# Memory keys and values of the second layer as one pair, with two seven-product places

## The chip, the cores and the metric

The kernel runs on one core of a Trainium2 chip. Its metric is the device time of one execution in microseconds, smaller is better, given as the median of several runs. The engines of the core are TensorE (PE: matmuls, and PEld: loads of the stationary operand), VectorE (DVE), ScalarE (ACT), GpSimd (POOL) and SyncE (SP, which here only issues DMAs). Matmuls write into PSUM, eight banks of 128 partitions by 512 fp32; everything else lies in SBUF or in the chip's memory.

## What is computed

The kernel is a decoder trunk of two layers for 256 tokens of width 2048. Both layers attend, besides their own mixer, to 256 memory tokens. The part that matters here is the projection of the normalized memory into keys and values, once for each layer:

```python
mem_n = rmsnorm(mem, norm_mem)
for i in range(DEPTH):                       # DEPTH = 2
    mk, mv = split_cols(mem_n @ mem_w_kv[i], [512, 512])   # mem_n 256x2048, each half 2048x512
    h = rmsnorm(x, norm_mix[i])
    x = x + mixer_i(h, mk, mv, ...)          # gated linear attention, then forgetting attention
    x = x + conv_ffn(rmsnorm(x, norm_ffn[i]), ...)
```

All of it is in fp32. TensorE gets each fp32 factor as a high and a low half, and a product is three matmuls: high by high, low by high, high by low.

## The kernel before

**Panels and units.** Every projection is cut into panels of at most 512 output columns. A panel has 16 blocks of 128 input features, loaded two at a time: a unit is 128 partitions by 2 x 512 weights (512 KB). For one unit TensorE runs 12 matmuls: two token halves, two feature blocks, three each. `proj_tm` (L235) runs one panel: `split_unit` (L211) loads a unit into `raw` (four buffers), ACT copies it to the high half `whi` (L208), DVE subtracts to get the low half `wlo` (L217; three buffers of each half), and `products` (L221) writes the matmuls of L229, L230 and L233. They collect in two `acc` banks out of a pool of four (L148), one for each token half, and after the last unit a panel's `evac` reads the banks.

**Pairs and seven-product places.** `proj_seven` (L270) runs two panels over the same input together, on all four banks, unit by unit in turn. At the units named in `forms` it takes the two units of the two panels as a 2 x 2 block problem (two token halves and two feature blocks, two panels) and uses seven products where eight would stand. It needs sums and differences of the weights (`t13` and `t24`, four DVE instructions, L338 to L341), their high and low halves (L312, L313), and sums of the tokens, made ahead (`summed`, L1022 to L1031). Three of the seven products go straight into `acc` banks, four into the work banks `m1`, `m5`, `m6`, `m7`, which are the kernel's `t`, `s` (two) and `o` banks, and `more` adds these up. All matmuls of a pair are written by `emit` (L286, the matmul is L291). Before the change only the down projections of the feed-forward do so, eight pairs with 20 places in all (`SEVEN`, L40).

**The memory stage.** L644 to L671 run four panels one after another on the memory tokens (`bufA`): keys and values of the first layer, then keys and values of the second, each by `proj_tm`. `keys` (L631) sends a panel through `to_features` (L420: scaled copy by ACT, transpose by DVE at L394, and two trips through memory); `mv_out` (L641) sends one through `to_values` (L442, the scaled copy is L449). The scales come from the memory norm: its squares are summed on tiles `x[0]` and `x[1]` (L646 to L654), a small matmul (L511) and a chain of short DVE instructions (L513 to L531, Newton steps at L519 to L522) follow when the norm is first asked for, at the evacuation of the first layer's values. Between the panels stand the 16 token splits for the next stage (L663, `split` at L468: an ACT copy with a gain, L478, and a DVE subtract, L479, from `xf` into `bufB`), the loads of the residual stream (`xtok` into `x`, L667, four of 512 KB) and its squares on ACT (`nx.add`, L559). After the stage the first panel of the gated linear attention (`gv`, 400 columns) reads `bufB` in order, two blocks a unit.

**What sets the order.** Each engine runs a fixed list. A planner writes the lists: it simulates the kernel and gives each engine at each moment the ready instruction of highest priority, which is that of the source, except that weight loads, casts and subtracts stand 300 places ahead (`AHEAD`, L39). `later` and `passed` (L178, L183) hang small steps on the count of units that have gone by, and `issue_after` holds a block behind a given instruction of the same engine (L665: behind the last weight load so far).

Of the kernel before, what the change touches and what calls it, by code (L numbers as in the profile page):

```python
# [19 lines left out]
P = 128  # L20
# [20 lines left out]
LAST = ()  # L41

# [95 lines left out]
def _trunk(ctx: ExitStack, tc: tile.TileContext, xt, xtok, memt, wp, wgu, gns, gfin, cnv, par, msk, out):  # L138
# [131 lines left out]
    def proj_seven(keys, src, forms, evacs, pool, more, early=False):  # L270

        units = [where[k] for k in keys]
        count = len(units[0])
        base = min(min(u[1]) for u in units[0])
        acc = [[pacc.tile([P, 512], F32, name="acc", tag="acc") for _ in range(2)] for _ in keys]
        m1, m5, m6, m7 = (work(t, n) for t, n in (("t", 1), ("s", 2), ("o", 1), ("s", 2)))
        begun, calls = set(), {}

        def form(a, x, hi, lo, c):
            s = slice(c * 512, (c + 1) * 512)  # L280
            out = []
            for xs, w in ((x[0], hi), (x[1], hi), (x[0], lo)):
                out.append((a, xs, w[:, s]))
            return out

        def emit(groups):  # L286
            todo = [g[n] for n in range(2) for g in groups] + [g[2] for g in groups]
            for a, x, w in todo:
                k = id(a)
                calls[k] -= 1  # L290
                TE.matmul(a, x, w, start=k not in begun, stop=calls[k] == 0)  # L291
                begun.add(k)
# [8 lines left out]
        for a in (m1, m5, m6, m7, acc[0][0], acc[1][0], acc[0][1]):  # L301
            count_calls(a, 3 * len(forms))
# [4 lines left out]
        def halves(raw, w):  # L307
            if w == NUNIT:
                hi, lo = (wpool.tile([P, w], F32R, name=n, tag=n, bufs=3) for n in ("whi", "wlo"))
            else:  # L310
                hi, lo = (pool.tile([P, w], F32R, name=n, tag=n) for n in ("vhi", "vlo"))
            casts.append(S.activation(hi, raw, AF.Copy))  # L312
            V.tensor_tensor(lo, raw, hi.bitcast(F32), ALU.subtract)  # L313
            return hi, lo

        def load(unit):
            off, kcs, n = unit
            raw = wpool.tile([P, NUNIT], F32, name="raw", tag="raw", bufs=4)
            loads.append(nc.sync.dma_start(raw, wp[off : off + P * NUNIT].rearrange("(p n) -> p n", p=P)))
            return raw  # L320

        for u in range(count):
            k0, k1 = units[0][u][1]
            if u not in forms:
                for i in range(2):
                    hi, lo = split_unit(units[i][u])
                    emit([form(acc[i][b], token(kc, b), hi, lo, c) for b in range(2) for c, kc in enumerate((k0, k1))])
                    if u == count - 1:
                        for b in range(2):
                            evacs[i](b, acc[i][b])  # L330
                if u == count - 2 and count - 1 in forms:
                    evacs[1](1, acc[1][1])
                continue
            s = forms[u]
            with tc.high_priority(offset=AHEAD + 40):
                r0, r1 = (load(units[i][u]) for i in range(2))
                t13, t24 = (pool.tile([P, 2, 512], F32, name=n, tag=n) for n in ("t13", "t24"))
                V.tensor_tensor(t13[:, 0, :], r1[:, :512], r0[:, :512], ALU.subtract)  # L338
                V.tensor_tensor(t13[:, 1, :], r1[:, 512:], r1[:, :512], ALU.subtract)
                V.tensor_tensor(t24[:, 0, :], r1[:, 512:], t13[:, 0, :], ALU.subtract)  # L340
                V.tensor_tensor(t24[:, 1, :], r0[:, 512:], t24[:, 0, :], ALU.subtract)  # L341
            with tc.high_priority(offset=AHEAD):
                v0 = halves(r0, NUNIT)
                v1 = halves(r1[:, 512:], 512)
            passed()
            emit([form(m1, token(k0, 0), *v0, 0), form(acc[0][0], token(k1, 0), *v0, 1)])
            emit([form(acc[1][0], s(3), *v1, 0)])
            with tc.high_priority(offset=AHEAD):
                v2 = halves(t13.rearrange("p c n -> p (c n)"), NUNIT)
            emit([form(m5, s(0), *v2, 0), form(m7, s(2), *v2, 1)])  # L350
            with tc.high_priority(offset=AHEAD):
                v3 = halves(t24.rearrange("p c n -> p (c n)"), NUNIT)
            passed()
            emit([form(m6, s(1), *v3, 0), form(acc[0][1], token(k1, 1), *v3, 1)])
            if u == count - 1:
                for i, b in ((0, 0), (1, 0), (0, 1)):
                    evacs[i](b, acc[i][b])
            if early and u == max(forms):
                more(m1, m5, m6, m7)

        if not early:
            more(m1, m5, m6, m7)

# [56 lines left out]
    def to_features(scales, dst, *steps):  # L420
# [3 lines left out]
        def evac(b, a):  # L424
# [3 lines left out]
            for k0, k1, s in scales:  # L428
# [3 lines left out]
                if s is None:  # L432
                    S.activation(o, i, AF.Copy)
                else:
                    S.activation(o, i, AF.Copy, scale=s()[:, b : b + 1])
            held[0].put(b, e)
# [5 lines left out]
    def to_values(norm, width, dst, more=None):  # L442
# [4 lines left out]
        def evac(b, a):  # L447
            e = tp.tile([P, 512], F32, name="scaled", tag="scaled", bufs=2)
            S.activation(e[:, :width], a[:, :width], AF.Copy, scale=norm.col()[:, b : b + 1])  # L449
            held.append(e)  # L450
# [158 lines left out]
    with tc.tile_pool(name="load", bufs=1) as lp:  # L609
# [46 lines left out]
        with tc.issue_after(loads[-1].ins):  # L656
            for i in range(KC):
                nc.sync.dma_start(xf[i], xt[i])
            nc.sync.dma_start(part, par)
            nc.sync.dma_start(mask[:, M_SCAN:], msk[:, M_SCAN:M_FOX])  # L660
        proj_tm(("mv", 0), bufA, mv_out(0))
        for i in range(KC):
            split(bufB, i, xf[i], gain("mix0", i), False)  # L663
        proj_tm(("mk", 1), bufA, keys(1))
# [6 lines left out]
        proj_tm(("mv", 1), bufA, mv_out(1))  # L671
# [295 lines left out]
    def add_seven(key, f, src, forms, pool, then=None):  # L967
# [13 lines left out]
        proj_seven([(*key, g) for g in (f, f + 1)], src, forms, [add_panel(g, then) for g in (f, f + 1)], pool, more,  # L981
                   then is not None)

    def ffn(l, nx, h, m, then, ending=None):
        with tc.tile_pool(name=f"ffn{l}", bufs=1) as fp, ExitStack() as ends:
# [11 lines left out]
            held = []  # L997

# [23 lines left out]
            def summed(form):  # L1022
                h0, h1 = (natural(h) for h in held)
                held.clear()
                f = sp.tile([P, 4, P], F32, name="sf", tag="sf")
                V.tensor_tensor(f[:, 0, :], h0[:, :, 1], h1[:, :, 1], ALU.add)
                V.tensor_tensor(f[:, 2, :], h0[:, :, 0], h0[:, :, 1], ALU.subtract)
                V.tensor_tensor(f[:, 1, :], f[:, 0, :], h0[:, :, 0], ALU.subtract)
                V.tensor_tensor(f[:, 3, :], h1[:, :, 0], f[:, 1, :], ALU.subtract)
                S.activation(form[:, 0, :, :], f, AF.Copy)  # L1030
                V.tensor_tensor(form[:, 1, :, :], f, form[:, 0, :, :].bitcast(F32), ALU.subtract)  # L1031
# [20 lines left out]
            for p, (lo, hi) in enumerate(PARTS):  # L1052
# [8 lines left out]
                if p < len(PARTS) - 1:  # L1061
                    for f, at in zip((0, 2), SEVEN):
                        add_seven(key, f, m, {u: form(forms[u]) for u in at}, sp)
                    continue
                if LAST:
                    add_seven(key, 0, m, {u: form(forms[u]) for u in LAST}, sp, then)
# [167 lines left out]
```

## Time and profile before

| what | value |
|---|---|
| median of 3 runs | 2243.26 us (2242.03 to 2243.55) |
| the profiled execution | 2244.32 us |
| its span, first to last instruction | 2242.5 us |
| mean granted TensorE clock | 0.999 |
| the four memory panels on TensorE | 5.37 to 95.53 us |
| of these, the second layer's keys and values | 51.43 to 95.53 us |

In the rows of the profile times are us from the start of the span unless marked ns. A row of a timeline has start, duration, engine, line, operation, output<-inputs, stationary and moving shapes, count, and in brackets the idle time before it with what ended it. A row of the groups has busy time and mean duration in ns of one instruction, and the idle time of the engine ahead of them. `wlo<-raw,whi` is a low half, `whi<-raw` a high half, `acc<-whi,A` a matmul on memory tokens, `acc<-whi,B` one on `bufB`. The duration of a matmul reaches into that of the next, so the pace is read from the starts.

### The profile page before, as it was taken

How to read it: one execution, taken by the hardware profiler on the slowest of the kernel's cores; microseconds unless marked ns; L12 is line 12 of the kernel's file. 1: busy time of each engine (PE TensorE's matmuls, PEld its weight loads, DVE VectorE, ACT ScalarE, POOL GpSimd, SP SyncE). 2: the span in 40 equal slices, each digit the busy share in tenths (PEclk: the TensorE clock that was granted, in tenths of full speed). 3: DMA queues.
4: the chain of work that ended last, by engine and by line, in shares of the span. 5: the costliest groups of instructions: out<-in, count | busy, mean ns of one | idle time of the engine just before them, and what ended most of it. 6: DMA issues, size and time to landing. Idle time of an engine off the chain costs nothing.

```text
span 2242.5 us, 29514 instructions
## 1 busy us (share of the span) xinstructions
PE 2229.0 (99%) x10276; PEld 1861.9 (83%) x10276; DVE 1631.0 (73%) x2553; ACT 1288.8 (57%) x1910; POOL 2.9 (0%) x15
## 2 busy tenths in 40 slices
PE   9999999999999999999999999999999999999998
PEld 7888888888888888888888998888888888888886
DVE  7568887667689677886776556666777967797766
ACT  7555666556565566555655555555665455654654
POOL 0000000000000000000000000000000000000000
PEclk9999999999999999999999999999999999999999
DMA  9876667677876777668787986677776678766774
GB/s 320 276 237 189 202 201 229 202 239 242 256 222 200 244 236 244 210 205 249 237 250 249 260 265 205 179 247 236 249 247 208 206 241 243 240 197 229 238 242 150
DMA packets 303773, 516.97 MB, mean 231 GB/s; under 512 B 178556, under 2 KB 187272, under 8 KB 303496
## 3 DMA queue, kind: packets, MB, share of 16 engines
q1 hardware_dynamic: 124296, 427.24, 59.1%
q10 hardware_dynamic: 179328, 87.85, 14.0%
q8 instruction: 80, 1.31, 0.3%
q14 instruction: 69, 0.57, 0.1%
HBM read 470.44 MB, written 44.58 MB: 230 GB/s over the span
## 4 chain that ended last, share of the span: by engine, by line
PE 96%; DMA 1%; DVE 1%; issue 0%; ACT 0%; SPq 0%; ACTq 0%; DVEq 0%
PE acc L229 26%; PE acc L230 26%; PE acc L233 26%; PE acc L291 12%; PE ps_s L291 1%; PE ps_o L291 1%; PE ps_t L291 1%; DMA xturned<-square 1%; PE ps_s L785 0%; DVE wlo L217 0%; PE ps_t L575 0%; PE ps_s L586 0%; PE ps_o L597 0%; DMA mt<-memt 0%; DMA raw<-wp 0%
## 5 line engine op out<-in xcount | busy, mean ns | idle before, releaser
L217 DVE TENSOR_TENSOR wlo<-raw,whi 128x1024 fp32r<-128x1024 f32 (+4 forms) x769 | 921.4, 1201 | 503.4 <-ACT whi L208 459.7
L208 ACT ACTIVATE whi<-raw 128x1024 fp32r<-128x1024 f32 (+4 forms) x769 | 799.0, 1041 | 741.1 <-PE acc L230 528.3
L229 PE MATMUL acc<-whi,B 128*128 128x512 f32 (+3 forms) x1536 | 586.2, 383 | 0.6 <-ACT whi L208 0.6
L230 PE MATMUL acc<-whi,B 128*128 128x512 f32 (+3 forms) x1536 | 584.9, 382 | 0.0
L229 PE MATMUL acc<-whi,A 128*128 128x512 f32 x1184 | 462.5, 392 | 0.9 <-ACT whi L208 0.6
L230 PE MATMUL acc<-whi,A 128*128 128x512 f32 x1184 | 461.2, 391 | 0.0
L233 PE MATMUL acc<-wlo,B 128*128 128x512 f32 (+3 forms) x1536 | 400.7, 381 | 0.0
L229 PEld LDWEIGHTS acc<-whi,B 128*128 128x128 f32 x1536 | 288.2, 188 | 51.5 <-ACT whi L208 1.1
L230 PEld LDWEIGHTS acc<-whi,B 128*128 128x128 f32 x1536 | 287.9, 188 | 49.7
L233 PEld LDWEIGHTS acc<-wlo,B 128*128 128x128 f32 x1536 | 285.6, 188 | 49.8
L233 PE MATMUL acc<-wlo,A 128*128 128x512 f32 x1184 | 318.5, 390 | 0.3 <-DVE wlo L217 0.3
L229 PEld LDWEIGHTS acc<-whi,A 128*128 128x128 f32 x1184 | 222.1, 188 | 49.2 <-ACT whi L208 2.4
L233 PEld LDWEIGHTS acc<-wlo,A 128*128 128x128 f32 x1184 | 222.1, 188 | 46.9 <-DVE wlo L217 0.7
L230 PEld LDWEIGHTS acc<-whi,A 128*128 128x128 f32 x1184 | 222.2, 188 | 46.1 <-DVE A L479 0.4
L1010 ACT ACTIVATE cv<-u,cw 128x256 f32<-128x256 f32 x176 | 96.8, 588 | 21.0 <-DMA u<-turned 21.0
L291 PE MATMUL acc<-whi,B 128*128 128x512 f32 x392 | 102.9, 390 | 0.3 <-ACT whi L208 0.3
L291 PE MATMUL acc<-whi,A 128*128 128x512 f32 x392 | 103.0, 390 | 0.0
L1011 DVE SCALAR_TENSOR_TENSOR cv<-u,cw,cv 128x256 f32<-128x256 f32 x176 | 78.4, 480 | 12.9 <-ACT cv L1010 12.9
L291 PEld LDWEIGHTS acc<-whi,B 128*128 128x128 f32 x392 | 73.5, 188 | 16.4 <-ACT whi L208 0.8
L291 PEld LDWEIGHTS acc<-whi,A 128*128 128x128 f32 x392 | 73.5, 188 | 16.1 <-ACT whi L208 0.4
L312 ACT ACTIVATE whi<-t 128x1024 fp32r<-128x1024 f32 x40 | 42.4, 1061 | 69.0 <-DVE t L341 35.3
L394 DVE STREAM_TRANSPOSE square<-scaled 128x512 f32<-128x512 f32 x122 | 79.9, 691 | 0.0
(231 smaller groups left out, 1604.0 us busy)
## 6 DMA issues: line engine op xcount, KB each, us to landing
raw<-wp SPq DMA_DIRECT2D x743, 512.0 KB, 4.3
turned<-square ACTq DMA_DIRECT2D x61, 512.0 KB, 4.3
u<-turned ACTq DMA_DIRECT2D x176, 128.0 KB, 5.1
raw<-wp SPq DMA_DIRECT2D x32, 384.0 KB, 3.5
raw<-wp SPq DMA_DIRECT2D x24, 388.0 KB, 4.6
back<-xturned ACTq DMA_DIRECT2D x64, 128.0 KB, 5.3
xturned<-square ACTq DMA_DIRECT2D x12, 512.0 KB, 4.0
back<-turned ACTq DMA_DIRECT2D x32, 128.0 KB, 4.6
```

The lines of the kernel that those rows point to most:

```text
L208: casts.append(S.activation(hi[:, s], raw[:, s], AF.Copy))
L217: V.tensor_tensor(lo[:, s], raw[:, s], hi[:, s].bitcast(F32), ALU.subtract)
L229: TE.matmul(acc[:, :n], xh, hi[:, s], start=first and j == 0, stop=False)
L230: TE.matmul(acc[:, :n], xl, hi[:, s], start=False, stop=False)
L233: TE.matmul(a, xh, ls, start=False, stop=stop)
L291: TE.matmul(a, x, w, start=k not in begun, stop=calls[k] == 0)
L312: casts.append(S.activation(hi, raw, AF.Copy))
L394: V.transpose(self.square[:, :, :, b], src.rearrange("p (c t) -> p c t", t=32))
L1010: S.activation(r, v[:, 2:], AF.Identity, bias=w[3], scale=w[2])
L1011: V.scalar_tensor_tensor(r, v[:, 1 : T + 1], w[1], r, ALU.mult, ALU.add)
```

## The change

The keys and values of the second layer no longer run as two panels but as one pair through `proj_seven`, with seven-product places at units 3 and 6 (`MEM_SEVEN`). A new `seven_evacuated` adds up the four work banks into SBUF after the last place, and the two evacuations add the sums by one DVE multiply-add for each bank, behind the scaled copy. `sums_of` makes the token sums of a place from the memory tokens, and is hung on the second and third unit of the pair. The scratch tiles are found rather than added where possible: high and low halves of the half unit in `bufB[15]` and `bufB[14]`, the two token sums in `bufB[10]` to `bufB[13]`, `t13` and `t24` in the tiles that later hold the second layer's keys and values; five tiles of 128x512 are new. Since six tiles of `bufB` are lent, the token splits 10 to 15 move behind the pair. The residual loads and their squares, which stood between the two panels, now stand ahead of the pair. `proj_seven` itself is made general (any width `n`, tiles from a callable) and takes the four work banks at the first place instead of at the start; `summed` and the new helper share `token_sums`.

```diff
+MEM_SEVEN = (3, 6)
...
-    def proj_seven(keys, src, forms, evacs, pool, more, early=False):
+    def proj_seven(keys, src, forms, evacs, tiles, more, early=False):
...
-        m1, m5, m6, m7 = (work(t, n) for t, n in (("t", 1), ("s", 2), ("o", 1), ("s", 2)))
...
+        shared = []
...
+            if not shared:
+                shared += [work(t, m) for t, m in (("t", 1), ("s", 2), ("o", 1), ("s", 2))]
+                for a in shared:
+                    count_calls(a, 3 * len(forms))
+            m1, m5, m6, m7 = shared
...
+    def seven_evacuated(keys, src, forms, evacs, tiles):
+
+        n = where[keys[0]][0][2]
+        extra = {}
+
+        def more(m1, m5, m6, m7):
+            u, v, w = (tiles(t, F32)[:, :n] for t in ("s16", "s165", "s1675"))
+            m1, m5, m6, m7 = (m[:, :n] for m in (m1, m5, m6, m7))
+            S.activation(u, m1, AF.Copy)
+            V.tensor_tensor(u, u, m6, ALU.add)
+            V.tensor_tensor(v, u, m5, ALU.add)
+            V.tensor_tensor(u, u, m7, ALU.add)
+            V.tensor_tensor(w, u, m5, ALU.add)
+            extra.update({(0, 0): m1, (1, 0): v, (0, 1): u, (1, 1): w})
+
+        def evac(i):
+            return lambda b, a: evacs[i](b, a, extra[i, b])
+
+        proj_seven(keys, src, forms, [evac(i) for i in range(2)], tiles, more, True)
+
+    def sums_of(src, chunks, f, h, form):
+
+        for c, k in enumerate(chunks):
+            V.tensor_tensor(h[:, c, :], *(src[k][:, i, :].bitcast(F32) for i in range(2)), ALU.add)
+        (a0, a1), (b0, b1) = ([h[:, c, b * P : (b + 1) * P] for b in range(2)] for c in range(2))
+        token_sums(a0, a1, b0, b1, f, form)
+
+    def token_sums(a0, a1, b0, b1, f, form):
+        V.tensor_tensor(f[:, 0, :], a1, b1, ALU.add)
+        V.tensor_tensor(f[:, 2, :], a0, a1, ALU.subtract)
+        V.tensor_tensor(f[:, 1, :], f[:, 0, :], a0, ALU.subtract)
+        V.tensor_tensor(f[:, 3, :], b0, f[:, 1, :], ALU.subtract)
+        hi, lo = form
+        S.activation(hi, f, AF.Copy)
+        V.tensor_tensor(lo, f, hi.bitcast(F32), ALU.subtract)
...
-        def evac(b, a):
+        def evac(b, a, extra=None):
...
+                    if extra is not None:
+                        V.scalar_tensor_tensor(o, extra, s()[:, b : b + 1], o, ALU.mult, ALU.add)
...
         proj_tm(("mv", 0), bufA, mv_out(0))
-        for i in range(KC):
-            split(bufB, i, xf[i], gain("mix0", i), False)
-        proj_tm(("mk", 1), bufA, keys(1))
+        for i in range(KC - taken):
+            tokens(i)
         with tc.issue_after(loads[-1].ins):
             for f in range(4):
                 nc.sync.dma_start(x[f], xtok[f])
         for f in range(4):
             for b in range(2):
                 nx.add(f, b)
-        proj_tm(("mv", 1), bufA, mv_out(1))
+        later(*[(2 + i, sums_at(u)) for i, u in enumerate(MEM_SEVEN)])
+        seven_evacuated([("mk", 1), ("mv", 1)], bufA, {u: picked(forms[u]) for u in MEM_SEVEN},
+                        [keys(1), mv_out(1)], lambda name, dtype: spots[name])
+        for i in range(KC - taken, KC):
+            tokens(i)
```

Here `taken` is 6, `tokens(i)` is the split of block i, and `spots` maps the names of the scratch tiles to the lent and the new tiles.

## What was predicted

> **What bounds the kernel now.** I read the page first: its line for the engines and the chain that ended last. Then the windows view for the stage that is edited, the timelines of each engine for its gaps, and the groups by line and shape for the prices.
>
> ```profile
> PE 2229.0 (99%) x10276; PEld 1861.9 (83%) x10276; DVE 1631.0 (73%) x2553; ACT 1288.8 (57%) x1910; POOL 2.9 (0%) x15
> ...
> PE 96%; DMA 1%; DVE 1%; issue 0%; ACT 0%; SPq 0%; ACTq 0%; DVEq 0%
> ```
>
> TensorE is busy for 2229.0 of 2242.5 us and is 96% of the chain. So a change can gain only by taking matmuls away or by closing one of the few gaps, which hold 13.5 us in the whole span; it loses when it opens a gap. The windows view shows the stage that is edited (the first layer's value panel, the two panels that become the pair, the panel behind them) and, as its last row, one feed-forward stretch that already runs five seven-product places.
>
> ```profile
> 28.40:51.07 22.67, 22.36 (x97) 17.85 (x97) 17.93 (x23) 14.31 (x20) 1.95 (x5) 1.00 0.95 300
> 51.43:95.53 44.10, 44.10 (x198) 36.50 (x196) 26.97 (x57) 25.32 (x53) 0.00 (x0) 1.00 0.83 278
> 95.53:112.96 17.43, 17.43 (x97) 17.43 (x96) 8.41 (x8) 8.35 (x11) 0.00 (x0) 1.00 0.84 262
> 642.00:726.00 84.00, 84.00 (x369) 68.76 (x368) 73.51 (x97) 46.70 (x56) 0.00 (x0) 1.00 0.65 208
> ```
>
> The columns behind the length are PE, PEld, DVE, ACT and POOL busy, granted clock, DMA share, GB/s. In the 44.10 us of the two second-layer panels TensorE never stops, while DVE has 26.97 and ACT 25.32: there is room to buy matmuls with DVE work. The last row says what such a purchase looked like: 369 matmuls (two pairs, 2 x 192 less 5 x 3), no idle TensorE, DVE at 73.51 of 84.00, or 88%. In the stage ahead (28.40 to 51.07) TensorE does lose a little, and the timelines of the three engines show where:
>
> ```profile
> 32.94 1.08 PE L233 MATMUL acc<-wlo,A 128*128 128x512 f32 x4
> 34.06 0.50 PE L229 MATMUL acc<-whi,A 128*128 128x512 f32 x1
> ...
> 35.78 0.39 PE L230 MATMUL acc<-whi,A 128*128 128x512 f32 x1
> 36.43 1.20 PE L233 MATMUL acc<-wlo,A 128*128 128x512 f32 x4 [0.26 <-DVE wlo L217]
> ```
>
> ```profile
> 33.27 0.84 DVE L479 SCALAR_TENSOR_TENSOR B<-xf,gains,B 128x256 fp32r<-128x256 f32 x2
> 34.02 1.22 DVE L651 TENSOR_TENSOR x<-x,x 128x1024 f32<-128x1024 f32 x1
> 35.16 1.22 DVE L217 TENSOR_TENSOR wlo<-raw,whi 128x1024 fp32r<-128x1024 f32 x1
> ```
>
> The low half of a weight unit (L217) stands behind two token splits (L479) and a square sum (L651), and the matmul at 36.43 waits for it.
>
> **The change, part by part.** The pace first, from the starts of whole units of 12 matmuls:
>
> ```profile
> 56.97 0.39 PE L229 MATMUL acc<-whi,A 128*128 128x512 f32 x1
> ...
> 59.69 0.39 PE L229 MATMUL acc<-whi,A 128*128 128x512 f32 x1
> ```
>
> 2.72 us for 12, so 0.227 us each. (The 0.39 in a row is a duration that overlaps the next.)
>
> *Matmuls.* A pair of units costs 24 matmuls; a seven-product place has 7 products of 3, so 21. Two places remove 6: **-1.36 us**, all of it on the path.
>
> *Token splits.* Six of sixteen leave the stretch from 24 to 37 us: 6 x 0.42 on DVE (two in 0.84 above) and as many casts on ACT. The two gaps above are 34.06 - 32.94 - 4 x 0.227 = 0.21, and 36.43 - 35.78 - 0.23 = 0.42. I take both as closed: **-0.63** (ends: -0.63, and 0 if other filler takes the place). The six land at the pair's end and in the panel behind, where DVE has 8.41 and ACT 8.35 of 17.43; the sixth unit there first reads them, some 11 us in. Hidden; without that cover 2.5 us of DVE work would be exposed.
>
> *DVE work of a place.* The rows of the feed-forward's own places:
>
> ```profile
> L313 DVE TENSOR_TENSOR wlo<-t,whi 128x1024 fp32r<-128x1024 f32 x40 | 48.6, 1224 | 11.4 <-ACT whi L312 8.6 <-PE acc L291 2.4
> ...
> L338 DVE TENSOR_TENSOR t<-raw 128x512 f32<-128x512 f32 x20 | 13.8, 692 | 10.8 <-DMA raw<-wp 10.5
> ...
> L313 DVE TENSOR_TENSOR vlo<-raw,vhi 128x512 fp32r<-128x512 f32 x20 | 13.7, 686 | 0.0
> ...
> L1031 DVE TENSOR_TENSOR forms<-sf,forms 128x512 fp32r<-128x512 f32 x12 | 8.3, 688 | 2.5 <-ACT forms L1030 2.5
> ...
> L972 DVE TENSOR_TENSOR x<-x,ps_t 128x512 f32<-128x512 f32 x8 | 5.5, 683 | 0.0
> ...
> L1027 DVE TENSOR_TENSOR sf<-cv 128x128 f32<-128x128 f32 x12 | 3.5, 289 | 0.0
> ```
>
> Per place: four differences (2.77), the half unit (0.69), three full low halves where two stood (+1.22): 4.68, twice 9.4. Token sums per place: two adds of 128x256 (0.84, as the two splits of that size), four of 128x128 (1.16), a low half (0.69): 2.7, twice 5.4. The combination behind the last place: four at 0.68, 2.7. The evacuation's four multiply-adds of 128x512 have no row; between the add's 0.68 (L972) and twice a 128x256 split's 0.42 I take 0.7: 2.8. Together 20.3. Instructions back to back overlap by some 0.07 (the 34 of them, 2.4), so 17.9 on top of 26.97: 44.9 in 42.7 us (44.10 less 1.36). That is too much, but not all of it is due there. The stream norm's chain,
>
> ```profile
> 71.08 0.17 DVE L564 TENSOR_REDUCE nm<-sums 128x2 f32<-128x16 f32 x1
> ...
> 78.41 0.16 DVE L522 TENSOR_TENSOR ny<-ny,nt 128x2 f32<-128x2 f32 x1
> ```
>
> 17 instructions of some 0.17 with two more behind them, 3.2 us, is needed only at the end of the panel behind (112.96), and the evacuation's 2.8 by nothing near: both can run in that panel. Due: 38.9 of 42.7, or 91%, a little above the feed-forward row, where TensorE lost nothing. **0**, with 2.2 as the end if nothing moves. ACT gains, per place, a full and a half cast and one of the sums, and one copy at the end; at DVE's prices, which are above ACT's (1.23 against 1.06 for a full unit), under 6 us on 25.32: no bound.
>
> *Loads.* The residual loads (four of 512 KB) were held behind the 24th weight unit and are now held behind the 16th, ahead of the pair's 16 units on SP's queue:
>
> ```profile
> 38.93 17.28 SPq L207 DMA_DIRECT2D raw<-wp  x9
> 56.27 1.89 SPq L667 DMA_DIRECT2D x<-xtok  x4
> ```
>
> ```profile
> 40.00:50.00 10.00, 10.00 (x46) 8.29 (x45) 5.55 (x7) 4.24 (x4) 0.00 (x0) 1.00 0.98 313
> ```
>
> There the DMA engines are 98% busy at 313 GB/s, so 2.1 MB push the weights back by up to 6.7 us. Of the pair's first units, the first and the third are cast at:
>
> ```profile
> 46.21 1.06 ACT L208 ACTIVATE whi<-raw 128x1024 fp32r<-128x1024 f32 x1 [1.29 <-DVE wlo L217]
> ...
> 50.36 1.06 ACT L208 ACTIVATE whi<-raw 128x1024 fp32r<-128x1024 f32 x1 [0.84 <-PE acc L230]
> ```
>
> They are used from 51.4 and 56.97, so the leads are 4.2 and 5.5 us. The queue fills gaps between weight loads, and the first residual tile cannot be written before the memory norm has read it (51.7), so I expect 1 MB (3.4 us) ahead of the first of them and 1.6 MB (5.0) by the third. **0**, with 6.7 - 4.2 = 2.5 as the other end. The 16 squares that follow on ACT move with them into a stretch where ACT has 4.24 of 10.
>
> *A new wait.* Two panels in turn used two of four accumulator banks each. The pair takes all four, so its second panel needs the banks of the first layer's values, and these are read only after the memory norm, whose chain starts when those values are done:
>
> ```profile
> 51.07 0.60 PE L511 MATMUL ps_t<-mask,x 128*128 128x128 f32 x4
> ...
> 54.25 0.39 PE L229 MATMUL acc<-whi,A 128*128 128x512 f32 x1
> ```
>
> ```profile
> 51.45 1.23 DVE L217 TENSOR_TENSOR wlo<-raw,whi 128x1024 fp32r<-128x1024 f32 x1 [0.68 <-ACT whi L208]
> 52.60 0.15 DVE L513 TENSOR_SCALAR nv<-ps_t 128x2 f32<-128x2 f32 x1
> ...
> 54.64 1.23 DVE L217 TENSOR_TENSOR wlo<-raw,whi 128x1024 fp32r<-128x1024 f32 x1 [0.29 <-ACT whi L208]
> ...
> 56.77 0.16 DVE L522 TENSOR_TENSOR ny<-ny,nt 128x2 f32<-128x2 f32 x1
> ```
>
> ```profile
> 57.23 1.25 ACT L449 ACTIVATE scaled<-acc,ny 128x512 f32<-128x512 f32 x2
> ```
>
> The banks come free at 57.9 and 58.5. The pair's second unit, in source order, would start at 54.25. But the order on TensorE is a planner's, and it mixes units where that helps; in a feed-forward pair the high halves of two units stand together (a unit has 8 such matmuls):
>
> ```profile
> 663.36 3.79 PE L291 MATMUL acc<-whi,A 128*128 128x512 f32 x16
> ```
>
> If it writes the keys' second unit ahead of the values' first, the need moves to 56.97 and, for the second bank, 57.42: a wait of **+1.0** (58.48 - 57.42). The ends are 0 (the norm chain without the weight subtract at 54.64 in its middle is 1.2 us shorter) and 58.48 - 54.70 = 3.8 (source order). Behind the waiting matmul stand all later ones; three weight buffers hold ACT's casts back with them, and they recover within the 5 us leads above.
>
> The Trainium skill, "TensorE: Matmul & The Clock Gate", section "Step-by-step: what each phase is for", says that matmuls stay in program order and only weight loads go ahead; by that nothing but the written order can fill this wait, and no run here shows it otherwise.
>
> *The rest.* The code that the feed-forward shares keeps its instructions; it only takes its four work banks at the first place instead of at the pair's start. 0.
>
> **Sum:** -1.36 - 0.63 + 1.0 = -1.0. The profiled execution took 2244.32, 1.06 above the median, its span 2242.5; the difference is set against the median: 2243.26 - 1.0 = **2242.3 us**.
>
> **Rivals.** (a) *No wait at the banks:* -2.0, 2241.3. For it: the chain waits 0.9 us ahead of 52.60 for one weight subtract and 1.2 in its middle for another, and DVE has fewer splits ahead of it. Against: the pair needs those low halves as early as before. (b) *The banks gate in source order:* 3.8 us, so -1.36 - 0.63 + 3.8 = +1.8, 2245.1. It turns slower once the wait passes 2.0 us. For it: the source order. Against: the feed-forward's mixed order. (b2) *The same wait also slows the matmuls behind it.* The trace's start shows a slow pace after idling:
>
> ```profile
> 1.45 3.61 PE L174 MATMUL ps_o<-B 128*128 128x512 f32 x8 [1.45 <-DVE B L171]
> ```
>
> That line is 0.45 us each, twice the later 0.227, over eight matmuls: 1.8 us extra, so 2246.9. The clock column would not tell, it reads 1.00 there too:
>
> ```profile
> 0.00:10.00 10.00, 7.93 (x24) 5.44 (x25) 4.39 (x8) 5.97 (x11) 0.30 (x5) 1.00 0.79 288
> ```
>
> The same page of the Trainium skill, section "Why this matters for your kernels", warns of idle gaps over about 3 us; only the start shows this here, no gap inside the span is that long. (c) *DVE or the loads fall short:* +2.2 or +2.5 on the sum, 2244.5 to 2244.8, or 2247.0 with both. (d) *The change reaches further than it says:* the shared code is written anew for the 8 feed-forward pairs too. Their matmuls wait for little now:
>
> ```profile
> PE acc L291 <- ACT whi L208: 0.3, 1, 0.3
> ...
> PE acc L291 <- DVE wlo L217: 0.3, 1, 0.3
> ```
>
> A better order can win back those 0.6 us; a worse one, with a wait of 0.3 at each of their 20 places, costs 6.0, so 2248.3.
>
> **How the numbers follow.** Forecast 0.44, (a) 0.20, (b) 0.12, (b2) 0.05, (c) 0.12, (d) 0.07. The range runs from (a) less 0.8 of scatter (2242.03 to 2243.55 is that of before) to (c) with both: 2240.5 to 2247.0. About 0.2% (4.5 us) is what a measurement of this kernel can tell from no change. Faster by that much needs three times the matmuls removed: 0.02, from causes that I can't name. Slower by that much takes (d), or two of (b), (b2) and (c) at once: 0.12. Within: 0.86.
>
> **What would show it.** 186 matmuls of 512 columns in the pair; no gap between 33 and 37 us; one gap of about 1 us some 5 us into the pair, released by ACT L449's line; residual loads near 40 us; DVE near 91% in the pair. Wrong would be: a gap of 3 us or more at that place, TensorE waiting for a low half at a place, or gaps in the feed-forward.

## The result, and the profile after

| kernel | median | lowest to highest | runs |
|---|---|---|---|
| before | 2243.49 us | 2241.16 to 2245.39 | 20 |
| after | 2246.90 us | 2244.39 to 2249.81 | 20 |

The ratio of the times is 1.0013, with a 95% interval of 1.0007 to 1.0019: slower by 2.9 us (1.6 to 4.3), within the 0.2% that was called no change, 4.6 us above the forecast and 0.1 below the top of its range.

One caution before the rows are read. The profiled execution of the changed kernel took 2244.39 us and was the fastest of its 20 runs; that of the kernel before took 2244.32, 0.8 above its median. So the two spans (2242.6 and 2242.5) look alike though the kernels are not. The loss is found in the edited stage, and two more traces of the changed kernel, among the experiments, show the usual execution.

The page of the changed kernel, line of the engines and of the chain:

```profile
PE 2226.6 (99%) x10270; PEld 1860.6 (83%) x10270; DVE 1646.0 (73%) x2587; ACT 1289.6 (58%) x1917; POOL 2.9 (0%) x15
...
PE 98%; DMA 1%; ACT 1%; DVE 0%; issue 0%; SPq 0%; ACTq 0%; DVEq 0%
```

Six matmuls are gone (10270 against 10276), and 2.4 us of TensorE's busy time with them; DVE has 15.0 us more. The windows of the changed kernel, cut at the same instructions as those of before (columns as in the prediction):

```profile
29.65:51.51 21.86, 21.86 (x98) 18.11 (x97) 14.31 (x15) 12.81 (x21) 0.00 (x0) 1.00 1.01 348
51.87:97.99 46.12, 43.48 (x191) 35.04 (x190) 40.19 (x83) 30.28 (x59) 0.00 (x0) 1.00 0.67 219
97.99:115.42 17.43, 17.43 (x96) 17.43 (x97) 11.68 (x15) 7.87 (x11) 1.95 (x5) 1.00 0.88 281
```

In the first row, the first layer's value panel, TensorE no longer stops. The second row is the pair. It has fewer matmuls than the two panels had, but takes 46.12 us instead of 44.10, and TensorE is busy for 43.48 of them: 2.64 us are idle that were not there before. Where they lie is shown by the view of the waits, here TensorE's in the changed kernel from 5 to 100 us (time in all, times, longest):

```profile
PE acc L292 <- ACT scaled L496: 2.2, 1, 2.2
PE acc L234 <- DVE wlo L218: 1.1, 1, 1.1
PE acc L230 <- ACT A L527: 0.5, 1, 0.5
PE acc L292 <- ACT whi L209: 0.2, 1, 0.2
...
PE acc L230 <- ACT scaled L480: 0.2, 1, 0.2
```

L496 is L449 of before, the scaled copy that empties the value banks; L218 is the low half (L217 before), L209 the cast (L208), L292 the matmul of a pair (L291). The first line is the wait that was forecast, at more than twice its size. The second, a low half, was not forecast. TensorE's timeline has both in their places:

```profile
18.97 0.39 PE L231 MATMUL acc<-whi,A 128*128 128x512 f32 x1
20.45 1.19 PE L234 MATMUL acc<-wlo,A 128*128 128x512 f32 x4 [1.10 <-DVE wlo L218]
...
36.77 0.39 PE L231 MATMUL acc<-whi,A 128*128 128x512 f32 x1
37.00 1.07 PE L234 MATMUL acc<-wlo,A 128*128 128x512 f32 x4
...
51.87 2.07 PE L292 MATMUL acc<-whi,A 128*128 128x512 f32 x8
...
57.81 2.11 PE L292 MATMUL acc<-whi,A 128*128 128x512 f32 x8 [0.24 <-ACT whi L209]
59.76 1.07 PE L292 MATMUL acc<-wlo,A 128*128 128x512 f32 x4
63.05 1.20 PE L292 MATMUL acc<-whi,A 128*128 128x512 f32 x4 [2.22 <-ACT scaled L496]
...
97.99 0.45 PE L230 MATMUL acc<-whi,B 128*128 128x400 f32 x1 [0.17 <-ACT scaled L480]
```

Counted from starts at the pace of 0.227 us, the stage up to the first matmul of the panel behind (97.99, before 95.53) adds up so: 1.26 at 19 us; -0.63 at 33 to 37 us, where the gaps are gone (37.00 follows 36.77 at the pace); -0.12 at the stage's start; 0.41 + 2.38 in the pair; 0.33 at its end; -1.36 for six matmuls. That is +2.27, and 97.99 - 95.53 = +2.46 was measured; the 0.2 between is spread too thin to be placed. Behind the stage the distance, matmul by matmul, first grows to 2.66 us, and then the two traces close up again: by 0.7 us between 240 and 320 us and 0.5 by 420 us, where the order of the planner puts the attention's small matmuls otherwise (1.40 us are left there), and by 1.3 more up to 1730 us, mostly where the profiled execution of before had two gaps of 0.47 and 0.50 at 1720 us that the changed kernel's did not have.

Why the banks came free so late is read on DVE and ACT. DVE's timeline of the changed kernel:

```profile
52.15 0.16 DVE L562 TENSOR_SCALAR nv<-ps_t 128x2 f32<-128x2 f32 x1 [2.21 <-PE ps_t L560]
...
52.83 1.22 DVE L218 TENSOR_TENSOR wlo<-raw,whi 128x1024 fp32r<-128x1024 f32 x1
...
54.04 0.69 DVE L407 TENSOR_TENSOR B<-plain,B 128x512 fp32r<-128x512 f32 x1
...
54.71 1.22 DVE L218 TENSOR_TENSOR wlo<-raw,whi 128x1024 fp32r<-128x1024 f32 x1
55.85 0.28 DVE L401 TENSOR_TENSOR plain<-plain 128x128 f32<-128x128 f32 x1
...
56.32 1.22 DVE L218 TENSOR_TENSOR wlo<-raw,whi 128x1024 fp32r<-128x1024 f32 x1
...
57.79 1.23 DVE L218 TENSOR_TENSOR wlo<-raw,whi 128x1024 fp32r<-128x1024 f32 x1
...
60.32 0.16 DVE L571 TENSOR_TENSOR ny<-ny,nt 128x2 f32<-128x2 f32 x1
```

The norm's chain (first `nv`, last `ny`) runs from 52.15 to 60.48, 8.3 us; before it took 4.3. Four low halves (4.9 us) and five instructions of the token sums (L401 to L404, L407: 1.8 us) stand between its short steps; in the chain of before stood one low half. Then ACT:

```profile
60.06 0.62 ACT L406 ACTIVATE B<-plain 128x512 fp32r<-128x512 f32 x1
60.58 1.04 ACT L209 ACTIVATE whi<-raw 128x1024 fp32r<-128x1024 f32 x1
61.53 0.40 ACT L608 ACTIVATE sq<-x 128x256 f32<-128x256 f32 x1
...
62.33 1.24 ACT L496 ACTIVATE scaled<-acc,ny 128x512 f32<-128x512 f32 x2
```

The scale is there at 60.48, the copy starts at 62.33. In front of it stand a cast and two squares of the residual stream (L608), which the change moved ahead of the pair together with the residual loads. Before, the copy followed the chain by 0.3 us.

### The profile page after: what moved, and what is told of

Its sections match the earlier page's. It is cut to its first block, busy times and chain, and to the rows that moved or that the text cites. A ratio compares the mean times of both kernels' runs of the same rounds, so it can differ in the third digit from the quotient of the medians.

```text
span 2242.6 us, 29548 instructions
## 1 busy us (share of the span) xinstructions
PE 2226.6 (99%) x10270; PEld 1860.6 (83%) x10270; DVE 1646.0 (73%) x2587; ACT 1289.6 (58%) x1917; POOL 2.9 (0%) x15
## 4 chain that ended last, share of the span: by engine, by line
PE 98%; DMA 1%; ACT 1%; DVE 0%; issue 0%; SPq 0%; ACTq 0%; DVEq 0%
PE acc L230 26%; PE acc L231 26%; PE acc L234 26%; PE acc L292 14%; PE ps_s L292 1%; PE ps_o L292 1%; PE ps_t L292 1%; PE ps_s L855 0%; DMA xturned<-square 0%; PE ps_t L624 0%; ACT whi L209 0%; PE ps_s L635 0%; PE ps_o L646 0%; DMA raw<-wp 0%; PE ps_s L997 0%
## 5 line engine op out<-in xcount | busy, mean ns | idle before, releaser
L218 DVE TENSOR_TENSOR wlo<-raw,whi 128x1024 fp32r<-128x1024 f32 (+4 forms) x765 | 914.7, 1199 | 470.0 <-ACT whi L209 439.3
L209 ACT ACTIVATE whi<-raw 128x1024 fp32r<-128x1024 f32 (+4 forms) x765 | 793.9, 1040 | 707.6 <-PE acc L231 479.8
L230 PE MATMUL acc<-whi,A 128*128 128x512 f32 x1120 | 437.1, 392 | 0.9 <-ACT A L527 0.5
L231 PE MATMUL acc<-whi,A 128*128 128x512 f32 x1120 | 436.4, 391 | 0.0
L234 PE MATMUL acc<-wlo,A 128*128 128x512 f32 x1120 | 301.4, 390 | 1.1 <-DVE wlo L218 1.1
L234 PEld LDWEIGHTS acc<-wlo,A 128*128 128x128 f32 x1120 | 210.1, 188 | 45.1 <-DVE wlo L218 1.5
L292 PE MATMUL acc<-whi,A 128*128 128x512 f32 x496 | 130.4, 391 | 2.7 <-ACT scaled L496 2.2
L292 PEld LDWEIGHTS acc<-whi,A 128*128 128x128 f32 x496 | 92.8, 188 | 23.6 <-ACT scaled L496 2.6
L292 PE MATMUL acc<-whi,B 128*128 128x512 f32 x392 | 102.9, 390 | 0.0
L292 PEld LDWEIGHTS acc<-whi,B 128*128 128x128 f32 x392 | 73.5, 188 | 15.9 <-ACT whi L209 0.2
```

The costliest lines, as they stand in the source:

```text
L209: casts.append(S.activation(hi[:, s], raw[:, s], AF.Copy))
L218: V.tensor_tensor(lo[:, s], raw[:, s], hi[:, s].bitcast(F32), ALU.subtract)
L230: TE.matmul(acc[:, :n], xh, hi[:, s], start=first and j == 0, stop=False)
L231: TE.matmul(acc[:, :n], xl, hi[:, s], start=False, stop=False)
L234: TE.matmul(a, xh, ls, start=False, stop=stop)
L292: TE.matmul(a[:, :n], x, w, start=k not in begun, stop=calls[k] == 0)
```

## The experiments

Theory: the loss is the wait at the value banks, made long by the token sums and squares in front of the norm's chain and its copy, plus the late low half at 19 us, which the token sums cause as well. Rivals: the loads that stand ahead of the pair; the pair order itself; the places' DVE work. No kernel leaves out part of the computation. "Panel behind" is the start of the first matmul with 400 columns in the kernel's own trace (95.53 before, 97.99 after).

| kernel | median | before beside it | ratio (95%) | panel behind |
|---|---|---|---|---|
| norm_early | 2243.54 | 2244.19 | 0.9996 (0.9988 to 1.0005) | 95.18 |
| sums_held | 2246.42 | 2244.19 | 1.0006 (0.9997 to 1.0015) | 99.51 |
| norm_sums | 2242.57 | 2244.19 | 0.9992 (0.9983 to 1.0001) | 94.94 |
| pair_only | 2245.39 | 2244.19 | 1.0005 (0.9996 to 1.0014) | 96.59 |
| after_look1, after_look2 | 2248.18, 2247.15 (one each) | 2244.22 | | 100.30, 99.23 |
| x_back | 2244.26 | 2244.22 | 0.9998 (0.9989 to 1.0007) | 96.84 |
| norm_x | 2240.54 | 2244.22 | 0.9983 (0.9974 to 0.9991) | 93.17 |
| pair_fixed | 2243.59 | 2243.61 | 1.0003 (0.9994 to 1.0012) | 95.50 |
| norm_x_free | 2242.04 | 2243.61 | 0.9991 (0.9982 to 1.0000) | 94.71 |
| before_norm | 2243.70 | 2243.61 | 0.9999 (0.9990 to 1.0008) | 95.61 |
| splits_only | 2245.62 (one) | 2243.61 | | 95.85 |

The medians are of 11 runs. The differences of one microsecond are read from the traces' stage; the ratios say whether the whole time agrees. One trace alone is no measure of the whole time: behind the stage some traces lose up to 2 us between 1270 and 1300 us that others do not (pair_only 2.0, before_norm 1.4, the traces of before and after none).

**norm_early: the chain is asked for two units before the value panel ends.**

```diff
+        later((6, nrm.col))
         proj_tm(("mv", 0), bufA, mv_out(0))
```

> The changed kernel, with the memory norm (small matmul and Newton chain) asked for at the sixth unit of the first layer's value panel instead of at that panel's evacuation. Theory (the values' banks wait for the norm, and the token sums that the planner put at 11 to 19 us delay a low half): the gap of 2.2 us in front of the pair's fourth unit goes, the one of 1.3 us near 19 us stays, so 2.5 to 2.8 under the changed kernel, about +0.6 on the kernel before (2243.5 to 2244.5). Rival 1 (the two places cost DVE more than they save): no change against the changed kernel, +3. Rival 2 (the residual loads ahead of the pair starve the weights): no change either, +3, with matmuls that wait for high halves.

DVE's and ACT's rows of this kernel:

```profile
48.32 0.15 DVE L562 TENSOR_SCALAR nv<-ps_t 128x2 f32<-128x2 f32 x1
...
52.13 0.16 DVE L571 TENSOR_TENSOR ny<-ny,nt 128x2 f32<-128x2 f32 x1
```

```profile
52.39 0.69 ACT L496 ACTIVATE scaled<-acc,ny 128x512 f32<-128x512 f32 x1 [3.10 <-DVE ny L571]
```

The chain is done at 52.29, the copy follows at once, and TensorE's units follow each other from 52.13 on with no gap in the pair but one of 0.19 that before has too. The 1.26 at 19 us stays, and at the pair's end 0.41 is lost. The panel behind starts at 95.18 instead of 97.99: 2.8 us, the two gaps in the pair. So the wait is that for the norm's chain and for what stood between it and the copy: with the chain early, all of it is gone.

**sums_held: the token sums wait for the latest low half on DVE.** `later` runs a step behind the last cast, but that holds only ACT's instruction of the sums; the planner is free to put DVE's part anywhere after the memory tokens exist.

```diff
+            def step():
+                with tc.issue_after(subs[-1].ins):
+                    sums_of(bufA, (2 * u, 2 * u + 1), plain[3].rearrange("p (i t) -> p i t", t=P),
+                            plain[4].rearrange("p (c t) -> p c t", t=T), forms[u])
+            return step
```

(`subs` collects the subtracts of L218.)

> The changed kernel, with the DVE part of the token sums held behind the low half of the unit they are hung on, as the source means it, instead of free to go to 11 to 19 us. Theory: the gap near 19 us (1.3 us) goes, but the sums (2 x 2 us of DVE) then stand in the norm's chain and the wait for the banks grows by 1 to 2 us: within 1 us of the changed kernel, +2.5 to +4 on before. Rival 1 (places too dear): as the changed kernel, with waits at the places. Rival 2 (loads): as the changed kernel, the gap near 19 us unmoved, since it would be the loads that make it.

In the changed kernel DVE's row ahead of the late low half was

```profile
11.59 0.75 DVE L396 TENSOR_TENSOR plain<-A 128x256 f32<-128x256 f32 x2
...
18.51 0.75 DVE L396 TENSOR_TENSOR plain<-A 128x256 f32<-128x256 f32 x2
19.18 4.62 DVE L218 TENSOR_TENSOR wlo<-raw,whi 128x1024 fp32r<-128x1024 f32 x4
```

that is, sums that TensorE first reads at 71.81, in a stretch where DVE has no idle time (14.00 of the 14 us from 10 to 24 us) and four low halves wait. With the sums held, the gap at 19 us is gone; TensorE's rows in the pair are now

```profile
57.89 2.14 PE L292 MATMUL acc<-whi,A 128*128 128x512 f32 x8 [1.66 <-ACT whi L209]
...
63.33 2.08 PE L292 MATMUL acc<-whi,A 128*128 128x512 f32 x4 [2.38 <-ACT scaled L496]
```

and nothing is won. By starts the waits are now 1.82 + 2.54 instead of 0.41 + 2.38. All of the sums stand in the chain's stretch, but the wait for the banks grows by less than the 1 to 2 us that were expected; the larger part is the late cast, for which ACT waits 2.21 us for a weight load (its row at 56.78). The second row shows something else: four matmuls in 2.08 us, where the changed kernel's first trace had 1.20. The windows of this kernel around it:

```profile
60.00:63.50 3.50, 1.12 (x6) 0.61 (x5) 3.11 (x12) 3.50 (x11) 0.00 (x0) 0.96 0.54 163
63.50:66.50 3.00, 3.00 (x8) 2.35 (x9) 3.00 (x9) 2.98 (x11) 0.00 (x0) 0.50 0.70 209
```

Behind the wait the granted clock is 0.50 for about 3 us: six to seven matmuls at 0.43 us instead of 0.227, 1.4 us.

**norm_sums: both.**

> Both edits at once: norm at the sixth unit of the value panel, token sums held. Theory: both gaps gone, six matmuls saved and the gaps at 33 to 37 us closed: -1.4 to -2.2 on before (2241 to 2242.2). Rival 1 (places too dear): +1 to +3, with waits for low halves at 70 to 90 us. Rival 2 (loads): +2 to +3.

Both gaps are gone together, 3.0 us earlier than the changed kernel. A new one opens at the first place: TensorE and DVE of this kernel,

```profile
72.20 0.50 PE L292 MATMUL ps_o<-whi,B 128*128 128x512 f32 x1 [0.96 <-ACT whi L315]
```

```profile
69.24 1.22 DVE L316 TENSOR_TENSOR wlo<-mk,whi 128x1024 fp32r<-128x1024 f32 x1
70.38 0.68 DVE L350 TENSOR_TENSOR mv<-raw,mv 128x512 f32<-128x512 f32 x1
```

The cast waits for a weight difference (L350) that DVE reaches at 70.38. So once nothing else delays the pair, a place can come late on DVE, here by 1.1 us.

**pair_only: the pair without places.** `MEM_SEVEN` is empty and the token sums are left out as the places are; the product is the usual eight.

```diff
-MEM_SEVEN = (3, 6)
+MEM_SEVEN = ()
...
-        later(*[(2 + i, sums_at(u)) for i, u in enumerate(MEM_SEVEN)])
```

> The changed kernel without the two places: the keys and values still run as a pair on all four banks, six token splits and the residual loads stand where the change put them, but every unit is plain (192 matmuls, no token sums, no extra evacuation). Theory: no gap near 19 us, a wait for the banks of 1 to 2 us (the chain is not stretched by sums, the squares on ACT are still there), and nothing saved: +0.5 to +1.5 on before. Rival 1 (places too dear): equal to before or faster, -0.6 to 0. Rival 2 (loads): +3, as the changed kernel.

The pair order alone costs 1.1 us in the stage, in two gaps of 0.37 and 0.42 at late casts (L209; ACT waits there for one of the three weight buffers). No wait at the banks is left, where 1 to 2 us were expected: without the token sums on DVE the chain ends at 57.34 instead of 60.48, and the copy starts at 57.75, with the squares behind it instead of in front. So the order of the pair did not have to cost a bank wait; what stands in front of the chain and the copy made it.

**after_look1, after_look2: the changed kernel twice more.**

> The changed kernel again, unchanged, for a second trace: its first trace (2244.4 us) is the fastest of twenty executions, the median is 2246.9. Theory (the wait for the values' banks; where it grows past some length the matmuls behind it run at half the pace, as in the trace of the kernel with the sums held, whose clock column reads 0.50 there): a time near 2247, the wait ahead of the pair's fourth unit above 2.2 us or followed by a stretch at half clock, 1 to 2 us more than in the first trace. Rival 1 (the rest lies in the later stages): the pair as in the first trace, gaps behind 400 us. Rival 2 (loads): the wait is for high halves that wait for DMA.

> As the look before it, a third trace of the changed kernel; the same is expected.

after_look2 has the same waits as the first trace to 0.01 us (0.24 and 2.22 in its rows), but not the same matmuls behind them. Its timeline and its window behind the wait:

```profile
63.01 1.71 PE L292 MATMUL acc<-whi,A 128*128 128x512 f32 x4 [2.22 <-ACT scaled L496]
64.52 1.05 PE L292 MATMUL acc<-wlo,A 128*128 128x512 f32 x2
65.38 1.78 PE L292 MATMUL acc<-whi,A 128*128 128x512 f32 x4
66.99 0.62 PE L292 MATMUL acc<-wlo,A 128*128 128x512 f32 x2
```

```profile
63.46:66.87 3.41, 3.41 (x10) 2.63 (x9) 3.31 (x10) 2.19 (x10) 0.00 (x0) 0.50 0.89 228
```

From 63.01 to 66.99 run ten matmuls, in 3.98 us; in the first trace the same ten ran from 63.05 to 65.45, in 2.40. That is 1.6 us; the panel behind starts 1.24 later (99.23 against 97.99), as the 0.33 at the pair's end is not there in this trace. In after_look1 the shorter wait was 1.28, the longer 2.57, and the clock column read 0.50 as well. So two of the three traces pay this, and the first trace, the fastest execution, does not. The timed runs point the same way: their mean granted clock reads 0.998 or less in 12 of 20 for the changed kernel and in 9 of 11 for sums_held, but in 19 of the 81 runs of before beside the experiments.

**x_back: the residual loads and squares go where the keys' panel had them**, that is, behind the eighth unit of the pair.

```diff
+        def residual():
             with tc.issue_after(loads[-1].ins):
                 for f in range(4):
                     nc.sync.dma_start(x[f], xtok[f])
             ...
+        later((8, residual))
```

> The changed kernel with the residual loads and their squares on ACT moved back, behind the pair's eighth unit. Theory (banks wait for the norm's chain; squares ahead of the evacuation on ACT lengthen it by 1.8 us, the loads by late weights): the wait for the banks falls to about 1 us and never reaches half clock; the gap near 19 us stays: 2244 to 2245.5, so 0 to +1.2 on before. Rival 1 (places too dear): 2246 to 2247. Rival 2 (loads alone): all of the loss goes, -1.4 to -2 on before.

TensorE's row at the banks:

```profile
62.21 1.19 PE L292 MATMUL acc<-whi,A 128*128 128x512 f32 x4 [1.09 <-ACT scaled L496]
```

The chain ends at 61.43 in this kernel, even later than in the changed one, but the copy starts 0.06 behind it (61.49) since no square stands before it, and the wait halves: 1.25 by starts, with no slow matmul behind. In whole time it equals before. The gap at 19 us stays. The squares, moved with their loads, are thus about half of the bank wait. That it is the squares is read from ACT's rows, since no run moves one without the other; against the first trace the loads show no cost (the smaller wait is 0.45 with and 0.41 without this edit), against after_look1 and sums_held they do (1.28 and 1.82, see below).

**norm_x: all three edits (norm_early, sums_held, x_back).**

> All three edits: the norm asked for early, the token sums held, the residual loads and squares behind the eighth unit. Theory: no gap near 19 us, none at the banks, none of 1 us at the first place (there DVE's queue was late with squares and sums): 2241 to 2242, -1.5 to -2.5 on before, 0 to 0.5 better than without the third edit. Rival 1: +1 to +3. Rival 2: as theory, so this run does not tell it.

TensorE's waits from 5 to 100 us, in all:

```profile
PE acc L230 <- ACT whi L209: 0.2, 1, 0.2
```

Everything that the change was to save is now saved: the panel behind starts 2.36 us before that of the kernel before, and by 420 us the trace leads by 3.5, as the attention behind it gets shorter here too, by 0.7 and 0.5. The 0.7 is luck of the planner's list: the changed kernel, sums_held, norm_x and norm_x_free have it, the other experiments do not. The time is 0.9983 (0.9974 to 0.9991) of before, 3.8 us and more than the 1.5 to 2.5 expected: this version beats both kernels. The forecast of rival (a), no wait at the banks, was 2.0, for the stage alone.

**pair_fixed, norm_x_free, before_norm: what each part of norm_x is worth.** pair_fixed is pair_only with norm_early's and x_back's edits; norm_x_free is norm_x without the hold on the sums; before_norm is the kernel before with norm_early's line.

> The fastest version so far (norm early, residual loads and squares behind the eighth unit) without the two places: a pair of plain units, 192 matmuls. Theory (TensorE is the bound once the waits are gone, so the places are worth their six matmuls, 1.4 us, and cost nothing): 1.4 above the version with places, 2241.5 to 2242.5. Rival (the places cost DVE more than they save): equal to it or faster, 2240 to 2241.

> The fastest version without holding the token sums: their DVE part is free to go to 11 to 19 us again. Theory: the gap of 1.25 us near 19 us is back and is all of the difference: 2241.5 to 2242.5. Rival (DVE has the time there, the gap came from the loads): equal to the version with the sums held, no gap near 19 us.

> The kernel before with the norm asked for early and nothing else. There the banks of the first layer's values are not needed until the fourth panel, so by theory it is worth nothing: within 0.7 of before. Rival (the early norm is a gain of its own, and the pair's fix only borrows it): 1.5 to 3 under before.

pair_fixed starts the panel behind at 95.50, before at 95.53: the pair by itself costs nothing once the chain, the squares and the loads are out of its way, and gains nothing. From there to norm_x it is 2.3 us: 1.36 of matmuls, 0.6 of the gaps at 33 to 37 us, which the lent tiles close, and 0.2 at 8 us, where the three traces of the changed kernel differ by as much. The whole times lie further apart than the 1.4 us that were expected (2243.59, outside its range, against 2240.54): the attention's 0.7 belongs to norm_x alone, and the rest is not placed. norm_x_free lacks 1.54 us in the stage, of which 1.25 is the low half at 19 us, back at 20.65 with 1.09 of idle time in its row.

before_norm is before: an early chain is worth nothing where no one waits for its banks.

**splits_only: before, with the last six token splits written behind the second value panel.**

```diff
-        for i in range(KC):
+        for i in range(KC - 6):
             split(bufB, i, xf[i], gain("mix0", i), False)
...
         proj_tm(("mv", 1), bufA, mv_out(1))
+        for i in range(KC - 6, KC):
+            split(bufB, i, xf[i], gain("mix0", i), False)
```

> The kernel before with the last six token splits moved behind the fourth panel and nothing else. Theory: the two gaps between 33 and 37 us (0.6 us) are gone in the trace, no new gap in the panel behind; the time is within the scatter. Rival (other filler takes their place): gaps of the same size there.

The two gaps stayed, 0.18 and 0.41, and pair_only and pair_fixed, which write the splits behind the pair too, keep them as well. The view of one line's instructions says why; first and last start stand behind the durations. In splits_only and then in the changed kernel:

```profile
L479 DVE SCALAR_TENSOR_TENSOR B<-xf,gains,B x16: 449/484/488, 24.2 to 37.0; 128x256 fp32r<-128x256 f32 x16
```

```profile
L528 DVE SCALAR_TENSOR_TENSOR B<-xf,gains,B x16: 471/476/489, 24.9 to 95.7; 128x256 fp32r<-128x256 f32 x16
```

Written later, all sixteen still run by 37 us, because their inputs and tiles are there and DVE has a free moment. In the changed kernel six run from 77.9 on, because their tiles are lent to the pair until then. So splits_only did not try what it was meant to try, and the gaps' closing is shown only together with the lent tiles.

## Why the prediction was wrong

**What bounds the kernel: right.** Matmuls and gaps on TensorE account for the stage to 0.2 us.

**Matmuls, -1.36: right.** 10276 to 10270, and in norm_x, with the gaps out of the way, the stage is shorter by 1.36 + 0.63 + 0.10 and 0.27 more.

**Token splits, -0.63: the size right, the reason half.** The gaps closed in the changed kernel. It was not the place in the source that closed them but the lending of the tiles (splits_only).

**"DVE work of a place", 0: wrong, +1.26.** The working compared DVE's total in the pair with the time there (38.9 of 42.7 us). It took for granted that the sums run where `later` hangs them. The planner put half of them at 11 to 19 us, where DVE is full, and the low half there came 1.26 us late; with DVE's part held (sums_held) that gap is gone. The end that was given, 2.2, covers it, but for another place. Inside the pair DVE's work did fit in the changed kernel; norm_sums shows how little room was left (1.1 us at the first place).

**"A new wait", +1.0: this is the step that failed most.** The mechanism was right in each part: the planner wrote the keys' units first, the banks of the first values gate the pair's second panel, and the release is the scaled copy. The size was 2.4, with 0.4 more at a late cast. The banks' side was 5 us later than forecast (62.33 + 0.69 = 63.02 for the first bank, against 57.9): the norm's chain started 0.45 earlier but was stretched on DVE from 4.3 to 8.3 us, and the squares and the cast ahead of the copy on ACT added 1.55. The need was later too, 60.67 instead of 56.97, as three units of the keys went ahead instead of two. The working had looked at the chain's length as before had it and even considered that it would get shorter; it did not ask which new instructions would be ready on DVE and ACT just then. Both kinds had been counted in the same text, the sums under DVE's work and the squares under the loads, and left out here.

**Rival (b2), half clock behind the wait: this did happen,** at less than the length of wait that was thought to call it, and in two of three traces. Its price, 1.4 us, is near the 1.8 worked out from the trace's start. The prediction held that the clock column would not tell it, as that column reads 1.00 over the start; inside the span the column did tell it, with 0.50. That the rival's sum of 2246.9 is the median to the decimal is chance: it took the 3.8 of rival (b) for the wait and no gap at 19 us, and in the measured kernel those are 2.8 and 1.26, less 1.1 that the attention behind the stage gives back by 420 us (2.46 to 1.40). The forecast's -1.0 with these put right (+1.8 of waits, +1.26, +1.4 of clock, -1.1 behind) is +2.4; 2.9 (1.6 to 4.3) was measured.

**Loads, 0: right in the first trace, too low in others.** Two residual tiles went at 37.42, one at 40.61 and the last only at 52.14, as expected behind the memory norm; ACT waited 1.79 us for a weight load at 50.48 in the changed kernel without TensorE noticing. But the weight load sent at 50 to 51 us, in front of the last residual tile, landed at 54.73 in the first trace, 56.51 in after_look2, 57.58 in after_look1 and 56.68 in sums_held, and at 54.11 in x_back, which has no residual loads there. In after_look1 and sums_held the late cast behind it cost TensorE 1.28 and 1.82 us instead of 0.41. So by the landings the loads added 0.9 and 1.4 us there; no run moves them alone, and which landing is the usual one stays open. **The shared code for the feed-forward, 0: right;** behind 600 us the matmuls of pairs wait 0.3 us in the changed kernel and 0.6 in before, at other places.

## What to carry to other kernels

When an edit makes an engine wait for a chain of short instructions, list every new instruction that is ready on the chain's engines in that stretch, and what stands ahead of the releasing one on its engine; the chain's length before is only its length in that company. In a planned order, the place in the source and a hook on one engine do not hold the work of another: only data, a buffer or an explicit hold on that engine does. Ask for a scale or a norm early if its only effect is to free a buffer, and read the first profile against the spread of the runs before explaining it.

## What the runs showed of the hardware

After a TensorE wait of 2.2 to 2.4 us in the rows, with another of 0.2 to 1.7 some 5 us before it, three of four traces had the granted clock at 0.50 for about 3 us (after_look1, after_look2, sums_held), at a price of 1.4 to 1.6 us on top of the wait; the first trace of the changed kernel, with the same waits, had 1.00, and x_back with 1.09 had 1.00.

What decides between the executions can be read from when the clock changes. In each of the fourteen traces the times of these changes lie a whole number of steps of 3.413 us apart: in after_look2 it falls to 0.50 at 63.46, is back at 66.87, one step on, and falls again at 2241.16, 637 steps later. The step that holds most of the wait, in after_look2, after_look1, sums_held, the first trace of the changed kernel and x_back, laid out from the last change of each trace:

```profile
60.04:63.45 3.41, 1.19 (x6) 0.69 (x5) 2.85 (x7) 3.41 (x10) 0.00 (x0) 1.00 0.70 264
60.49:63.90 3.41, 1.33 (x6) 0.75 (x4) 2.56 (x7) 3.41 (x12) 0.00 (x0) 1.00 0.62 232
59.84:63.25 3.41, 1.10 (x5) 0.56 (x3) 3.02 (x10) 3.41 (x12) 0.00 (x0) 1.00 0.57 172
59.11:62.52 3.41, 1.72 (x8) 1.09 (x6) 2.72 (x10) 3.41 (x13) 0.00 (x0) 1.00 0.85 303
59.09:62.50 3.41, 2.32 (x10) 1.61 (x10) 2.89 (x8) 2.50 (x4) 0.00 (x0) 1.00 1.03 418
```

Where TensorE was busy for 1.10 to 1.33 us of the step, the next step had half clock; where it was busy for 1.72 or 2.32, it had not. The first trace has the same wait as after_look2, but there it reaches over the end of a step. So in these five traces it is the share of a step that counts and not the length of the wait alone; where between 1.33 and 1.72 us the limit lies, no run shows. The Trainium skill, "TensorE: Matmul & The Clock Gate", section "Why this matters for your kernels", puts the limit at idle gaps of more than about 3 us; here shorter ones sufficed, and the measurement decides. The same page, section "What's actually happening", says that the activity window runs freely and does not start with the kernel's work; the traces agree, as the steps begin at another offset from the span's start in each (the step above at 59.11 in the first trace, at 60.04 in after_look2).
